# A decoder block on one core: token squares and decay columns later, the branch's split five gate tiles later, embedding norms from copies, the last two norms in two parts

## The chip, the cores and the metric

The kernel runs on one core of a Trainium2 chip. The time is the device time of one execution in microseconds (us), lower is better. TensorE multiplies matrices (its weight loads have their own row in the profile, PEld), VectorE (DVE), ScalarE (ACT) and GpSimd (POOL) do elementwise work, SyncE (SP) and POOL issue the DMA transfers. Matmul results lie in PSUM, in eight banks of 512 float32 columns; everything else lies in SBUF.

## The reference: one decoder layer

For a residual stream x of 512 tokens by 1024 channels the reference computes, in float32:

```
h = rms_norm(x, g_mix_pre);  z = h @ w_in          # 1024 -> 512 + 1024 + 1024 + 2048
y_pool = pool_mixer(z_pool) @ w_pool_out           # trailing means over 2, 4, 8, 16 tokens minus the token,
                                                   # each group through its 128x128 pool_w
y_rnn  = rg_lru_branch(z_rx, z_rg) @ w_rg_out      # conv of 4 taps, gates r and i, decay a = exp(-8 r softplus(-lambda)),
                                                   # linear scan over the tokens, times gelu(z_rg)
x = x + rms_norm((sigmoid(z_g1)*y_pool + sigmoid(z_g2)*y_rnn) @ w_o, g_mix_post)
up = rms_norm(x, g_ffn_pre) @ w_up                 # 1024 -> 2 x 3072
hid = gelu(causal_dwconv(up[:3072])) * up[3072:]
x = x + rms_norm(hid @ w_down, g_ffn_post)
ple = rms_norm(p @ w_ple_proj, g_ple_post)         # p: 512 x 256, the embedding of this layer
x = x + sigmoid(rms_norm(x, g_ple_gate) @ w_ple_gate) * ple
```

rms_norm divides by the root of the mean square over the 1024 channels of a token and multiplies by a gain. The reciprocal roots are called rstd below.

## The kernel before, in words

**Three passes for each product.** Every operand is split into two float32r numbers: `hi`, which is ScalarE's cast of the value, and `lo`, which is VectorE's difference between the value and `hi` (the subtraction in `sub`, line 189, called from `split` and from `prep`). A product is then three matmuls, hi by hi, hi by lo and lo by hi (`mm3`, lines 219 to 221). So each weight tile costs a DMA load by SP, a cast on ACT (line 433) and a subtraction on DVE (line 189) before TensorE may use its `lo`. `weight(key, ahead)` calls `prep` for so many tiles ahead of the one asked for, in the order of one list. The w_o, up and down products run as seven products of half-size blocks in place of eight, with sums and differences of the blocks formed in DRAM, in SBUF or in PSUM.

**What sets the order.** The program is written in one stream and a scheduler sorts each engine's instructions by priority; `tc.high_priority` and `urgent` move a stretch ahead, and `behind(ins, name)` forbids an instruction to stand ahead of another one of the same engine. Each engine then runs its list strictly in that order, so an instruction that waits holds up all that stand behind it.

**Start (lines 479 to 525).** SP loads x transposed in eight tiles of 256 KB (`m`, "x0" to "x7" below) and the four weight tiles of the recurrent input (`rx`, 512 KB). ACT scales each x tile into `hi` (line 487), DVE makes its `lo` (line 488), and TensorE runs eight steps k of twelve matmuls into four banks (line 524). Between these, SP loads x by tokens as well, in two transfers of 1 MB (`C<-x`, line 493), and ACT squares and sums them (line 507, four instructions). From the sums come the rstd of the tokens (POOL, line 455), and four diagonal matrices of them on DVE (line 515), which TensorE spreads to all partitions (line 569) in the first tile of the next product. On the same lines of work stand the decay columns `sp` of the recurrence, some 24 operations on 128x8 numbers on DVE and two on ACT (lines 544 to 563).

**Input projections (lines 578 to 750).** Twelve tiles `in` give the recurrent branch, then a written order `IN_ORDER` runs gate tiles, pool tiles and pool maps in turn. A gate or pool tile is 24 matmuls of 512 columns. A pool map is three matmuls: it multiplies the 128x128 block of `pool_w` (`hi_1423`, `lo_1424`) with the split trailing mean of a group. When the scans are done, `rnn_split` splits the eight results of the branch into `hi` and `lo` (the `C` tiles, eight casts and eight DVE subtractions); it is called behind gate tile 0.

**Mixer output and embedding (lines 765 to 1075).** Behind the w_o products come four tiles of the embedding (`ple_tile`, line 757): two products of 12 matmuls into two banks, a copy of one bank by DVE (line 769) and of the other by ACT (line 770), squares of both banks by ACT (line 462, in `rstd_of`), rstd on POOL, and the stores of the copies to DRAM. All squares but those of the start are kept in program order by `last_square`. Around these lie the norm of x after the mixer (`x2_sum`, `x2_out`: DVE lines 871, 874, 947) and the transposes of h2 on TensorE (line 879).

**End (lines 1188 to 1277).** `x3_norm(t, pair)` ends the down product for each tile of 128 tokens: `add_norm` multiplies both halves by the gain (line 871, two banks or a bank and an SBUF sum), squares both, takes the rstd and adds to the residual (line 874); then x3 times the next gain goes to `h` (line 1185), its squares give `r3`, and `x3_tile` transposes it on TensorE (line 879) and splits it. The last products run for h=0 and h=1, over t = 0 to 3, with the weights `wpg`, whose `lo` for h=1 is four DVE subtractions of 128x1024. `ple` tiles are multiplied by `rp` and the gain on DVE (line 1258), the sigmoid of the product is multiplied with them (1270), added to x3 (1271) and stored.

## Time and profile before

| what | before |
|---|---|
| three runs | 710.96, 711.29, 712.65 us; median 711.29 us |
| profiled execution | 712.31 us, of it span 710.3 us from the first to the last instruction |
| TensorE matmul | 699.5 us busy (98%), 4281 instructions |
| TensorE weight load | 637.0 us (90%) |
| VectorE | 576.6 us (81%) |
| ScalarE | 441.0 us (62%) |
| GpSimd | 82.3 us (12%) |
| DMA | 172.53 MB, mean 243 GB/s |

A busy time is the sum of an engine's instructions and does not say whether something waited for it. In a row of the timeline the first two numbers are start and duration in us; "xN" joins N neighbours of one kind; the bracket gives idle time before the row and what released it. In the list of waits the three numbers are total us, times, longest us. A matmul of 512 columns starts 0.216 us behind the one before it where nothing holds it, one of 256 columns 0.111 us; durations of matmuls overlap, so gaps are read from starts.

### The profile page before, as it was taken

The page shows a single profiled execution, that of the slowest core. Times are in us where ns is not written, and L with a number is a line of the kernel's source. Part 1 is how long each engine was busy: PE and PEld are TensorE (multiplying, and loading weights), DVE is VectorE, ACT ScalarE, POOL GpSimd, SP SyncE. Part 2 cuts the span into 40 slices and gives each one's busy share as a digit, 9 for nine tenths or more (in the row PEclk, how much of TensorE's full clock was granted, in tenths as well). Part 3 has the DMA queues.
Part 4 walks back from the last instruction along what each step waited for, and adds up shares of the span by engine and source line. Part 5 has one row for each costly group of instructions (what it writes and reads, how often), then busy time and mean ns, then how long its engine had stood idle before and what let it go on. Part 6 is the DMA issues. An engine that isn't in the chain of part 4 may idle for free.

```text
span 710.3 us, 11245 instructions
## 1 busy us (share of the span) xinstructions
PE 699.5 (98%) x4281; PEld 637.0 (90%) x4281; DVE 576.6 (81%) x749; ACT 441.0 (62%) x670; POOL 82.3 (12%) x107
## 2 busy tenths in 40 slices
PE   9999999999999999999999999999999999999897
PEld 7888888888888888889999999999999888888786
DVE  3897745999756578776989899899999999789852
ACT  6756789854643245487866677666667766574721
POOL 0311111110000000120013222222200000010100
PEclk9999999999999999999999999999999999999999
DMA  8999787765698999995379999999967677868011
GB/s 318 386 314 279 189 237 162 179 150 189 235 345 271 318 339 357 334 327 187 124 261 267 263 310 251 317 241 337 230 196 232 202 248 229 282 194 290 7 60 59
DMA packets 64933, 172.53 MB, mean 243 GB/s; under 512 B 5808, under 2 KB 6448, under 8 KB 64560
## 3 DMA queue, kind: packets, MB, share of 16 engines
q1 hardware_dynamic: 50336, 129.78, 52.7%
q0 software_dynamic: 14400, 41.95, 25.1%
q8 instruction: 33, 0.54, 0.3%
q14 instruction: 20, 0.16, 0.1%
q10 hardware_dynamic: 144, 0.10, 0.1%
HBM read 155.03 MB, written 58.72 MB: 301 GB/s over the span
## 4 chain that ended last, share of the span: by engine, by line
PE 75%; DVE 12%; ACT 5%; DMA 3%; issue 2%; POOL 1%; SPq 0%; DVEq 0%; POOLq 0%; ACTq 0%
PE ps L219 25%; PE ps L220 25%; PE ps L221 24%; DVE lo L189 3%; ACT m L164 1%; DMA C<-in_x_dram 1%; POOL s L455 1%; DVE m L656 1%; ACT t L164 1%; ACT rb L462 1%; DVE C L189 1%; DMA m<-in_x_t_dram 1%; DVE m L947 1%; PE ps L627 1%; DVE A L1258 1%
## 5 line engine op out<-in xcount | busy, mean ns | idle before, releaser
L189 DVE TENSOR_TENSOR lo<-raw,hi 128x1024 fp32r<-128x1024 f32 (+2 forms) x193 | 224.3, 1184 | 54.3 <-ACT hi L433 40.1
L219 PE MATMUL ps<-A,hi 128*128 128x256 f32 (+1 forms) x608 | 194.5, 320 | 0.0
L220 PE MATMUL ps<-A,hi 128*128 128x256 f32 (+1 forms) x608 | 193.8, 319 | 0.0
L221 PE MATMUL ps<-A,lo 128*128 128x256 f32 (+1 forms) x608 | 193.8, 319 | 0.0
L433 ACT CAST hi<-raw 128x1024 fp32r<-128x1024 f32 (+1 forms) x112 | 112.3, 1010 | 94.4 <-PE ps L220 28.3
L219 PEld LDWEIGHTS ps<-A,hi 128*128 128x128 f32 x608 | 115.9, 191 | 8.4 <-issue 1.3
L221 PEld LDWEIGHTS ps<-A,lo 128*128 128x128 f32 x608 | 116.0, 191 | 6.9
L220 PEld LDWEIGHTS ps<-A,hi 128*128 128x128 f32 x608 | 116.0, 191 | 6.7
L219 PE MATMUL ps<-C,hi 128*128 128x256 f32 (+1 forms) x392 | 114.7, 293 | 1.5 <-ACT rb L462 1.2
L220 PE MATMUL ps<-C,hi 128*128 128x256 f32 (+1 forms) x392 | 114.3, 291 | 0.0
L221 PE MATMUL ps<-C,lo 128*128 128x256 f32 (+1 forms) x392 | 114.3, 291 | 0.0
L193 ACT CAST hi<-raw 128x1024 fp32r<-128x1024 f32 x78 | 80.5, 1050 | 20.5 <-PE ps L220 12.2
L219 PE MATMUL ps<-hi,A 128*128 128x512 f32 x224 | 85.3, 381 | 0.0
L220 PE MATMUL ps<-lo,A 128*128 128x512 f32 x224 | 84.9, 379 | 0.0
L221 PE MATMUL ps<-hi,A 128*128 128x512 f32 x224 | 84.9, 379 | 0.0
L219 PEld LDWEIGHTS ps<-C,hi 128*128 128x128 f32 x392 | 74.7, 190 | 3.9 <-ACT rb L462 1.5
L220 PEld LDWEIGHTS ps<-C,hi 128*128 128x128 f32 x392 | 74.7, 191 | 1.8
L221 PEld LDWEIGHTS ps<-C,lo 128*128 128x128 f32 x392 | 74.7, 191 | 1.7
L455 POOL TENSOR_TENSOR s<-s,mhalf 128x1 f32<-128x1 f32 (+1 forms) x21 | 15.7, 749 | 343.0 <-DVE s L468 323.1
L219 PEld LDWEIGHTS ps<-hi,A 128*128 128x128 f32 x224 | 42.3, 189 | 6.3 <-ACT hi L433 0.3
L221 PEld LDWEIGHTS ps<-hi,A 128*128 128x128 f32 x224 | 42.3, 189 | 6.0
L220 PEld LDWEIGHTS ps<-lo,A 128*128 128x128 f32 x224 | 42.3, 189 | 5.9
(191 smaller groups left out, 1024.7 us busy)
## 6 DMA issues: line engine op xcount, KB each, us to landing
raw<-in_w_up_dram SPq DMA_DIRECT2D x46, 512.0 KB, 8.1
wdsum<-in_w_down_dram POOLq DMA_DIRECT2D x36, 512.0 KB, 9.1
raw<-in_w_in_dram SPq DMA_DIRECT2D x32, 512.0 KB, 7.1
raw<-wdsum SPq DMA_DIRECT2D x24, 512.0 KB, 4.2
raw<-in_w_down_dram SPq DMA_DIRECT2D x18, 512.0 KB, 4.4
wosum<-in_w_o_dram POOLq DMA_DIRECT2D x12, 512.0 KB, 9.7
wdsum<-wdsum POOLq DMA_DIRECT2D x12, 512.0 KB, 8.0
parts<-hi SPq DMA_DIRECT2D x10, 512.0 KB, 5.0
```

Of the source, the lines that this page charges most:

```text
L164: ins = ACT.activation(o, i, func, **kw)
L189: V.tensor_tensor(o, a, b, ALU.subtract)
L193: last_copy[0] = ACT.copy(hi, src)
L219: PE.matmul(o, ah, bh, start=start, stop=False, **kw)
L220: PE.matmul(o, ah, bl, start=False, stop=False, **kw)
L221: PE.matmul(o, al, bh, start=False, stop=stop, **kw)
L433: ACT.copy(hi, raw)
L455: last_pow[0] = nc.gpsimd.tensor_tensor(y, v, mhalf[:, :n], ALU.pow).ins.name
L462: ins = ACT.activation(rb, hsrc, AF.Square, scale=1.0 / 32.0, accum_out=s)
L627: PE.matmul(ps, bd[pr, a, o], turns(b[pr]), start=i == 0, stop=i == 2)
L656: V.tensor_tensor_scan(r, a_t[c], r, 0.0, ALU.mult, ALU.add)
L947: V.scalar_tensor_tensor(h2n[t, h], res[h], r, g_pre[h], ALU.mult, ALU.mult)
```

## The change

Five edits, which leave the sums and products as they are:

1. The two loads of x by tokens move behind the loads of the last weight tile and of x7; their squares may not stand ahead of the scaling of x5 (the first) and x7 (the other three). The four diagonals move behind `lo` of the weight tile `in` 0. The decay columns become a function that is called behind the third `in` tile.
2. `rnn_split` is called behind gate tile 5 in place of gate tile 0.
3. In the embedding the squares read the copies in SBUF in place of the banks, in a function `ple_norm` that is called behind the x2 work of the same tile; they leave the common order of squares.
4. `x3_norm` is split: `norm_of` squares one half while DVE multiplies the other half by the gain, and takes the rstd; `x3_add` does the rest. For t=2 and t=3 both adds come behind both `norm_of`, and the adds of t=2 not ahead of the last gain multiply of t=3.
5. The `ple` multiplies of t=2 and 3 may not stand ahead of the last multiply of x3; casts and subtractions of `wpg` for h=1 may not stand ahead of the last cast and the last subtraction of a `split`; the lookahead of `wpg` is cut to 3 - k//2 tiles for h=0, t=0 and 1.

```diff
-        V.tensor_tensor(o, a, b, ALU.subtract)
+        return V.tensor_tensor(o, a, b, ALU.subtract)
...
+        last_low[0] = sub(lo, src, hi.bitcast(F32)).ins.name
...
-            ACT.copy(hi, raw)
+            ins = ACT.copy(hi, raw)
+            if key[0] == "wpg" and key[2] == 1:
+                behind(ins, last_copy[0].ins.name)
...
-                sub(lo, raw, hi.bitcast(F32))
+                ins = sub(lo, raw, hi.bitcast(F32))
+                low_of[key] = ins.ins.name
+            if key[0] == "wpg" and key[2] == 1:
+                behind(ins, last_low[0])
...
+    def square(v, in_order=True):
+        s = tiny()
+        ins = ACT.activation(rb, v, AF.Square, scale=1.0 / 32.0, accum_out=s)
+        if in_order:
             if last_square[0] is not None:
                 behind(ins, last_square[0])
             last_square[0] = ins.ins.name
+        return s
...
+    def rstd_from(sums):
         v = tiny()
         V.scalar_tensor_tensor(v, sums[0], EPS, sums[1], ALU.add, ALU.add)
         return rsqrt(v)
...
         if k % 2 == 1 and k < 7:
-            if k > 1:
-                xt = quad("C", F32)
-                a = k // 2 - 1
-                nc.sync.dma_start(
...
             weight(("rx", k // 2 + 1), ahead=0)
+        if k in (5, 7):
+            load_tokens(k // 2 - 2)
...
+    last_func[0] = ht_done[-1]
...
-            ACT.activation(v, v, AF.Square, scale=1.0 / 32.0, accum_out=ssq[:, t : t + 1])
+            behind(ACT.activation(v, v, AF.Square, scale=1.0 / 32.0, accum_out=ssq[:, t : t + 1]), ht_done[7 if t else 5])
...
+        behind(V.tensor_scalar(diag[:, t * P : (t + 1) * P], ident, rstd1[:, t : t + 1], None, ALU.mult), low_of["in", 0])
...
+        if n == 2:
+            decay_columns()
...
-        if m == 0:
+        if m == 5:
             rnn_split()
...
-        s = rstd_of(pair)
...
+    def ple_norm(t, outs):
+        s = rstd_of(outs, in_order=False)
...
-            ple_tile(t)
+            outs = ple_tile(t)
...
+        ple_norm(t, outs)
...
+    def norm_of(pair, g):
+        og, sums = [temp(), temp()], []
+        for h in range(2):
+            sums.append(square(pair[h]))
+            ins = V.tensor_tensor(row(og[1 - h]), back(pair[1 - h]), row(g[1 - h]), ALU.mult)
+        return og, rstd_from(sums), ins.ins.name
...
+    def x3_add(t):
+        og, r, done = x3_first[t]
         res = [x3[t // 2][:, 2 * (t % 2) + h, :] for h in range(2)]
         with tc.high_priority(offset=URGENT if t > 1 else 0):
-            add_norm(pair, (gq[:, 0, :], gq[:, 1, :]), res)
+            norm_add(og, r, res, x3_first[3][2] if t == 2 else None)
...
+        if q == NQ + 1:
+            x3_add(2)
+            x3_add(3)
...
-            V.scalar_tensor_tensor(v, v, rp[t], gp[:, h, :], ALU.mult, ALU.mult)
+            ins = V.scalar_tensor_tensor(v, v, rp[t], gp[:, h, :], ALU.mult, ALU.mult)
+            if t > 1:
+                behind(ins, x3_last[0])
...
-                    w = weight(("wpg", k // 2, h))
+                    w = weight(("wpg", k // 2, h), ahead=AHEAD if h or t > 1 else 3 - k // 2)
```

TensorE's and POOL's instructions keep their order. On SP the two token loads and a few stores and loads behind the mixer change places. What moves on ACT and DVE is shown at three places. In a row stand line, operation, the output and the inputs; the numbers of buffers and lines differ between the two programs.

At the start, on ACT before (`A` is the scaling of an x tile, `C,s` a token square, the casts are those of rx tiles):

```order
L487 ACTIVATE A_131<-m_137,col 128x512
L487 ACTIVATE A_131<-m_138,col 128x512
L507 ACTIVATE C_173,s_201<-C_173 128x1024 x2
L433 CAST hi_177<-raw_175 128x1024
L487 ACTIVATE A_132<-m_139,col 128x512
L487 ACTIVATE A_132<-m_140,col 128x512
L507 ACTIVATE C_187,s_201<-C_187 128x1024 x2
L433 CAST hi_191<-raw_189 128x1024
L487 ACTIVATE A_132<-m_141,col 128x512
L487 ACTIVATE A_132<-m_142,col 128x512
```

and in the changed program:

```order
L506 ACTIVATE A_131<-m_137,col 128x512
L506 ACTIVATE A_131<-m_138,col 128x512
L433 CAST hi_175<-raw_173 128x1024
L506 ACTIVATE A_132<-m_139,col 128x512
L506 ACTIVATE A_132<-m_140,col 128x512
L433 CAST hi_187<-raw_185 128x1024
L521 ACTIVATE C_191,s_201<-C_191 128x1024
L506 ACTIVATE A_132<-m_141,col 128x512
L506 ACTIVATE A_132<-m_142,col 128x512
L521 ACTIVATE C_191,s_201<-C_191 128x1024
L521 ACTIVATE C_199,s_201<-C_199 128x1024 x2
L433 CAST hi_272<-raw_270 128x1024
```

The squares of the first two token tiles stood ahead of the rx cast and of x4 and x5, the other two ahead of the next rx cast and of x6 and x7. Now one square stands behind x5 and three behind x7.

On DVE around the first pool map, before (`C_1142` and `C_1152` are the low parts of the branch, `lo_1424` that of `pool_w`, `m_1304` that of the first pool group, `t` its running sums):

```order
L189 TENSOR_TENSOR C_1152<-m_996,C_1151 128x512
L189 TENSOR_TENSOR C_1152<-m_1002,C_1151 128x512
L712 TENSOR_TENSOR t_1297<-t_1294 128x512
L189 TENSOR_TENSOR lo_1424<-raw_1421,hi_1423 128x512
L189 TENSOR_TENSOR lo_1472<-raw_1469,hi_1471 128x1024
L189 TENSOR_TENSOR lo_1506<-raw_1503,hi_1505 128x1024
L717 SCALAR_TENSOR_TENSOR t_1299<-t_1297,t_1294 128x511
...
L189 TENSOR_TENSOR lo_1556<-raw_1553,hi_1555 128x1024
L189 TENSOR_TENSOR m_1304<-t_1299,m_1303 128x512
```

and in the changed program, where the low part of the first pool group is called `m_1284`:

```order
L189 TENSOR_TENSOR C_1402<-m_807,C_1401 128x512
L730 TENSOR_TENSOR t_1357<-t_1355 128x512
L189 TENSOR_TENSOR m_1284<-t_1279,m_1283 128x512
L599 TENSOR_TENSOR m_1318<-ps_1293,rb 128x512
...
L189 TENSOR_TENSOR m_1364<-t_1359,m_1363 128x512
L599 TENSOR_TENSOR m_1398<-ps_1373,rb 128x512
L189 TENSOR_TENSOR C_1412<-m_996,C_1411 128x512
L189 TENSOR_TENSOR C_1412<-m_1002,C_1411 128x512
L189 TENSOR_TENSOR lo_1424<-raw_1421,hi_1423 128x512
L189 TENSOR_TENSOR lo_1472<-raw_1469,hi_1471 128x1024
L189 TENSOR_TENSOR lo_1506<-raw_1503,hi_1505 128x1024
```

Before, all eight low parts of the branch stood ahead of the first pool group's chain, and `lo_1424` with two weights inside that chain. Now the chain of group 0 and most of that of group 1 (`t_1359`, `m_1364`) is interleaved with the low parts of the branch, `m_1284` stands ahead of the last five of these, and `lo_1424` and the four weights behind them all.

On DVE at the end, before, from the gain multiplies of t=3 on (`t<-ps` and `t<-sum`) to its `h` and the split of its transposes:

```order
L871 TENSOR_TENSOR t_6926<-ps_2822,C_5963 128x512
L871 TENSOR_TENSOR t_6928<-sum_6326,C_5963 128x512
L468 SCALAR_TENSOR_TENSOR s_6875<-s_6871,s_6873 128x1
L189 TENSOR_TENSOR lo_6958<-raw_6955,hi_6957 128x1024
L1188 COPY r_6879<-s_6877 128x1
L189 TENSOR_TENSOR lo_6970<-raw_6967,hi_6969 128x1024
L468 SCALAR_TENSOR_TENSOR s_6934<-s_6930,s_6932 128x1
L874 SCALAR_TENSOR_TENSOR C_6695<-t_6926,s_6936,C_6695 128x512
L874 SCALAR_TENSOR_TENSOR C_6695<-t_6928,s_6936,C_6695 128x512
L1185 TENSOR_TENSOR h_6809<-C_6695,C_5963 128x512 x2
L189 TENSOR_TENSOR h_7019<-ps_7020,h_7019 128x512
L189 TENSOR_TENSOR h_7019<-ps_7027,h_7019 128x512
```

and in the changed program, from the sum of squares of t=2 to the `h` of t=3 (`t_6912` and `t_6913` are the gain multiplies of t=3):

```order
L474 SCALAR_TENSOR_TENSOR s_6863<-s_6857,s_6860 128x1
L891 TENSOR_TENSOR t_6913<-sum_6326,C_5963 128x512
L189 TENSOR_TENSOR h_6867<-ps_6875,h_6867 128x512
L189 TENSOR_TENSOR lo_6903<-raw_6900,hi_6902 128x1024
L891 TENSOR_TENSOR t_6912<-ps_2822,C_5963 128x512
L896 SCALAR_TENSOR_TENSOR C_6695<-t_6855,s_6865,C_6695 128x512
L896 SCALAR_TENSOR_TENSOR C_6695<-t_6856,s_6865,C_6695 128x512
L1221 TENSOR_TENSOR h_6809<-C_6695,C_5963 128x512 x2
L474 SCALAR_TENSOR_TENSOR s_6920<-s_6914,s_6917 128x1
L896 SCALAR_TENSOR_TENSOR C_6695<-t_6912,s_6922,C_6695 128x512
L896 SCALAR_TENSOR_TENSOR C_6695<-t_6913,s_6922,C_6695 128x512
L1221 TENSOR_TENSOR h_6809<-C_6695,C_5963 128x512 x2
```

The weight subtractions `lo_6958` and `lo_6970`, which are the first for h=1, no longer stand between the gain multiplies of t=3 and its add, the gain multiplies of both tiles stand ahead of the adds of t=2, and the adds of both tiles follow one another.

More of the change, by code (lines that the diff above doesn't have):

```diff
@@ L456, in rsqrt @@
         return y
-    def rstd_of(halves):
-        sums = []
-        for hsrc in halves:
-            s = tiny()
-            ins = ACT.activation(rb, hsrc, AF.Square, scale=1.0 / 32.0, accum_out=s)
+    def square(v, in_order=True):
+        s = tiny()
+        ins = ACT.activation(rb, v, AF.Square, scale=1.0 / 32.0, accum_out=s)
+        if in_order:
             if last_square[0] is not None:
@@ L469, in rstd_of @@
         return rsqrt(v)
+    def rstd_of(halves, in_order=True):
+        return rstd_from([square(v, in_order) for v in halves])
     hth = [quad("A"), quad("A")]
@@ L479, in block_kernel, with load_tokens @@
     xtok = []
+    ht_done = []
+    def load_tokens(a):
+        xt = quad("C", F32)
+        nc.sync.dma_start(
+            xt.rearrange("p (a h) c -> p a (h c)", a=2),
+            x[2 * a * P : 2 * (a + 1) * P, :].rearrange("(a p) c -> p a c", p=P),
+        )
+        xtok.append(xt)
     for k in range(KD):
@@ L486, in block_kernel @@
         hi, lo = ht(k)
-        ht_done = ACT.activation(hi, raw, AF.Identity, scale=c1(C_GMIX + k)).ins.name
+        ht_done.append(ACT.activation(hi, raw, AF.Identity, scale=c1(C_GMIX + k)).ins.name)
         V.scalar_tensor_tensor(lo, raw, c1(C_GMIX + k), hi.bitcast(F32), ALU.mult, ALU.subtract)
         if k % 2 == 1 and k < 7:
-            if k > 1:
-                xt = quad("C", F32)
-                a = k // 2 - 1
-                nc.sync.dma_start(
-                    xt.rearrange("p (a h) c -> p a (h c)", a=2),
-                    x[2 * a * P : 2 * (a + 1) * P, :].rearrange("(a p) c -> p a c", p=P),
-                )
-                xtok.append(xt)
             weight(("rx", k // 2 + 1), ahead=0)
+        if k in (5, 7):
+            load_tokens(k // 2 - 2)
+    last_func[0] = ht_done[-1]
     ssq = tiny(NT)
@@ L512, in block_kernel @@
     sum_in_dram(chain_of(sums_of("wo"), sums_of("up")), None)
-    diag = temp()
-    for t in range(NT):
-        V.tensor_scalar(diag[:, t * P : (t + 1) * P], ident, rstd1[:, t : t + 1], None, ALU.mult)
     rx = [bank() for _ in range(4)]
@@ L524, in block_kernel @@
                 PE.matmul(rx[m], a[:, o : o + P], turns(b), start=k == 0 and i == 0, stop=k == KD - 1 and i == 2)
+    diag = temp()
+    for t in range(NT):
+        behind(V.tensor_scalar(diag[:, t * P : (t + 1) * P], ident, rstd1[:, t : t + 1], None, ALU.mult), low_of["in", 0])
     bd = quad("C").rearrange("p (s a) c -> p s (a c)", s=2)
@@ L770, in ple_tile @@
         ACT.copy(row(outs[1]), back(pair[1]))
-        s = rstd_of(pair)
+        for h, o in enumerate(outs):
+            nc.sync.dma_start(pled[t * P : (t + 1) * P, h * S : (h + 1) * S], o)
+        return outs
+    def ple_norm(t, outs):
+        s = rstd_of(outs, in_order=False)
         rp[t] = const.tile([P, 1], F32, tag=f"rp{t}", name=f"rp{t}")
         V.tensor_copy(rp[t], s)
-        for h, o in enumerate(outs):
-            nc.sync.dma_start(pled[t * P : (t + 1) * P, h * S : (h + 1) * S], o)
     def product(name, lhs, f, banks, start, head=0, tail=0):
@@ L864, in block_kernel, with norm_add @@
                 split(*pq[k], raw)
-    def add_norm(pair, g, res):
-        og = []
-        for h in range(2):
-            og.append(temp())
-            V.tensor_tensor(row(og[h]), back(pair[h]), row(g[h]), ALU.mult)
-        r = rstd_of(pair)
-        for h in range(2):
-            V.scalar_tensor_tensor(res[h], og[h], r, res[h], ALU.mult, ALU.add)
+    def norm_of(pair, g):
[4 more added lines that the diff above has]
+        return og, rstd_from(sums), ins.ins.name
+    def norm_add(og, r, res, after=None):
+        for h in range(2):
+            ins = V.scalar_tensor_tensor(res[h], og[h], r, res[h], ALU.mult, ALU.add)
+            if after is not None:
+                behind(ins, after)
+    def add_norm(pair, g, res):
+        og, r, _ = norm_of(pair, g)
+        norm_add(og, r, res)
     def transposed(a):
@@ L1177, in block_kernel @@
     x3n = {}
+    x3_first, x3_last = {}, [None]
     def x3_norm(t, pair):
+        with tc.high_priority(offset=URGENT if t > 1 else 0):
+            x3_first[t] = norm_of(pair, (gq[:, 0, :], gq[:, 1, :]))
+    def x3_add(t):
+        og, r, done = x3_first[t]
         res = [x3[t // 2][:, 2 * (t % 2) + h, :] for h in range(2)]
         with tc.high_priority(offset=URGENT if t > 1 else 0):
-            add_norm(pair, (gq[:, 0, :], gq[:, 1, :]), res)
+            norm_add(og, r, res, x3_first[3][2] if t == 2 else None)
             for h in range(2):
                 x3n[t, h] = nq[t // 2][:, 2 * (t % 2) + h, :]
-                V.tensor_tensor(x3n[t, h], res[h], gq[:, 2 + h, :], ALU.mult)
+                x3_last[0] = V.tensor_tensor(x3n[t, h], res[h], gq[:, 2 + h, :], ALU.mult).ins.name
         s3 = rstd_of(res)
@@ L1236, in block_kernel @@
             x3_norm(1, (c11[1], c12[1]))
+            x3_add(1)
             nq[1], gp = hquad(), hquad()
```

48 lines of the change are left out of this document (24 added, 24 removed).

## The prediction

> **What bounds the kernel now.** I read the page first, then TensorE's waits, then the timeline around each of them.
>
> ```profile
> PE 699.5 (98%) x4281; PEld 637.0 (90%) x4281; DVE 576.6 (81%) x749; ACT 441.0 (62%) x670; POOL 82.3 (12%) x107
> ```
> ```profile
> PE ps L879 <- DVE h L1185: 1.7, 1, 1.7
> PE ps L219 <- ACT rb L462: 1.2, 1, 1.2
> PE ps L237 <- DVE mhalf L231: 1.1, 1, 1.1
> PE ps L220 <- DVE m L189: 0.9, 1, 0.9
> PE ps L524 <- DVE lo L189: 0.7, 1, 0.7
> ```
>
> TensorE is the bound, and its list of matmuls does not change. All the change can win is stalls. There are few: the four rows beside the first wait of the program (L237) are one stall each, in four stages: the end, the embedding, the first pool map, the start. A stall costs its gap and then about 0.10 us, since the first matmul behind it starts its successor 0.32 us later in place of 0.216 (162.03 to 162.35 below). So each part is priced at its own stall, from starts of matmuls. I give all times on the clock of the profile before.
>
> **Part 1, the start.**
>
> ```profile
> 16.13 1.03 PE L524 MATMUL ps<-A,hi 128*128 128x512 f32 x4
> 17.35 1.13 PE L524 MATMUL ps<-A,hi 128*128 128x512 f32 x4 [0.20 <-ACT A L487]
> ...
> 21.77 1.90 PE L524 MATMUL ps<-A,hi 128*128 128x512 f32 x8
> 24.35 1.13 PE L524 MATMUL ps<-A,lo 128*128 128x512 f32 x4 [0.68 <-DVE lo L189]
> ```
> ```profile
> 13.55 1.06 ACT L507 ACTIVATE C<-C 128x1024 f32<-128x1024 f32 x1 [1.62 <-DMA C<-in_x_dram]
> ...
> 18.74 1.06 ACT L507 ACTIVATE C<-C 128x1024 f32<-128x1024 f32 x1 [0.83 <-DMA C<-in_x_dram]
> ```
> ```profile
> 22.28 0.88 DVE L515 TENSOR_SCALAR t<-ident,s 128x128 f32<-128x128 f32 x4 [1.15 <-POOL s L455]
> 23.08 1.21 DVE L189 TENSOR_TENSOR lo<-raw,hi 128x1024 fp32r<-128x1024 f32 x1
> ```
>
> Four matmuls from 16.13 make the next due at 16.99; it starts at 17.35, because x4's scaling stands behind two squares that waited for the token load (13.55). Eight from 21.77 make the next due at 23.50; it starts at 24.35, because the low part of the last rx tile (23.08) stands behind the diagonals, which waited for the second token load (18.74), two squares and POOL. Loss 0.36 + 0.85 + twice 0.10 = 1.4 us.
> Afterwards: between the rows 13.55 and 18.74 landed one rx tile, x4, x5 and the second token tile, 2 MB in 5.2 us, so 0.65 us per 256 KB. Without the first token load ahead of them (2.6 us), in the new order rx2 lands at 12.25, x4 12.9, x5 13.55, rx3 14.85, tokens 17.45, x6 18.1, x7 18.75, tokens 21.35. x4, x5 and rx3 are then scaled, cast and subtracted by 17.2, long before 22.2; both stalls go. What is late next: the diagonals. Two squares end at 23.45, DVE's sum and POOL take 1.4 (POOL's idle of DVE above is 1.15), so rstd is there at 24.8; two weight subtractions of 1.1 each stand ahead, three diagonals are done at 27.8, the fourth behind one more at 29.1. TensorE spreads them behind the twenty matmuls from 24.35 on and nine of the next product: 24.35 - 1.3 + 29 x 0.216 = 29.3. Margin 0.2, so the gain is 1.4, at worst 1.0. The 24 operations of the decay columns go to a stage in which DVE has idle time and gates start some 20 us later: nothing.
> The rows above agree with transfers that land in the order of issue. The Trainium skill, "DMA: Bandwidth & Descriptors", section "Queues, rings and completion order", says that completion is not first in, first out per issuing engine, and its section "Issuing engines are not separate DMA queues" that transfers interleave; by that the order of the loads alone would guarantee none of these landings. No row of this profile shows a load that overtakes another; the case in which one does is the third rival below.
>
> **Part 2, the branch's split.**
>
> ```profile
> 149.79 4.90 DVE L189 TENSOR_TENSOR C<-m,C 128x512 fp32r<-128x512 f32 x8
> ...
> 155.21 2.96 DVE L189 TENSOR_TENSOR lo<-raw,hi 128x512 fp32r<-128x512 f32 x3
> ```
> ```profile
> 160.74 0.38 PE L219 MATMUL ps<-m,hi 128*128 128x512 f32 x1
> 162.03 0.48 PE L220 MATMUL ps<-m,hi 128*128 128x512 f32 x1 [0.92 <-DVE m L189]
> 162.35 0.38 PE L221 MATMUL ps<-m,lo 128*128 128x512 f32 x1
> ```
> ```profile
> 130.00:165.00 35.00, 34.08 (x159) 29.52 (x158) 34.89 (x59) 20.86 (x32) 4.12 (x5) 1.00 0.70 186
> ```
>
> DVE is busy 34.89 of these 35 us: it is a queue that only order can shorten. The map's second matmul waits for `m_1304`, the last of its chain; due at 160.96, it starts at 162.03. With the new order `m_1284` comes early. Counting from 149.79, where the same work has been done in both, nine 512-wide rows at 0.61 (4.90/8) and two or three short ones stand up to and with `m_1284`: done by 155.7, five us before it is wanted. But the map's third matmul needs `lo_1424`, and this now stands behind all eight low parts and both chains: twenty 512-wide rows and some ten short ones, 20 x 0.61 + 0.4 = 12.6, so 162.4 where it was done by 155.9 (155.21, the first of the three). The third matmul, due at 161.17, runs at 162.35 as before. The wait changes its name and keeps its length. Then the next gate tile needs its own `lo_1472`, 1.13 later, at 163.5, where its third matmul was due at 163.0. So this part is no gain: -0.1 to -0.5, I take -0.4. Bounds: -0.6 with the restart, and +1.2 if the low parts are done early enough after all.
>
> **Part 3, the embedding norms.**
>
> ```profile
> 316.31 0.38 PE L221 MATMUL ps<-hi,m 128*128 128x512 f32 x1
> 316.89 0.38 PE L219 MATMUL ps<-C,hi 128*128 128x256 f32 x1 [0.21 <-ACT m L905]
> ```
> ```profile
> 322.68 0.71 PE L879 MATMUL ps<-ident,m 128*128 128x128 f32 x5
> 324.64 0.38 PE L219 MATMUL ps<-C,hi 128*128 128x256 f32 x1 [1.25 <-ACT rb L462]
> ```
> ```profile
> 323.09 1.28 DVE L769 COPY m<-ps 128x512 f32<-128x512 f32 x2
> ```
> ```profile
> 323.89 0.60 ACT L462 ACTIVATE rb<-ps 128x512 f32<-128x512 f32 x1 [2.02 <-DVE m L769]
> ```
>
> The 324.64 matmul writes a bank that is free only behind a copy on DVE (323.09) and then a square on ACT (323.89). The transposes' last start is near 323.12, so some 1.4 us go, 0.37 more at 316.89, and 0.1 for each restart: 2.0. With squares from the copies a bank is free once it is copied. What is late next are the copies themselves. ACT's copy of the last pair but one now stands behind two squares of the tile before, and I count it done at 322.3; DVE's keeps its place behind the norm's multiplies, so the first of the two at 323.09 ends at 323.7. TensorE, without its stalls, takes these two banks at 322.8 and 324.1. Margins of 0.5 and 0.4, and by the same count 0.3 at 316.9. I take 1.8 of the 2.0, and 1.0 if both slip. A square of a copy in SBUF is priced by the token squares of the start, 1.06 for 1024 columns, so 0.53 for 512, against 0.60 from a bank (323.89): no more than now, and ACT waits there anyway (2.02).
>
> **Part 4, the end.**
>
> ```profile
> 657.58 0.69 DVE L871 TENSOR_TENSOR t<-ps,C 128x512 f32<-128x512 f32 x1
> ...
> 671.08 1.41 DVE L874 SCALAR_TENSOR_TENSOR C<-t,s,C 128x512 f32<-128x512 f32 x2 [0.72 <-POOL s L455]
> 672.41 1.29 DVE L1185 TENSOR_TENSOR h<-C,C 128x512 f32<-128x512 f32 x2
> ```
> ```profile
> 665.06 0.38 PE L220 MATMUL ps<-lo,h 128*128 128x512 f32 x1
> 665.52 0.48 PE L221 MATMUL ps<-hi,h 128*128 128x512 f32 x1
> ```
> ```profile
> 671.03 0.38 PE L221 MATMUL ps<-hi,h 128*128 128x512 f32 x1
> 673.15 1.10 PE L879 MATMUL ps<-ident,h 128*128 128x128 f32 x6 [1.74 <-DVE h L1185]
> ```
>
> Stalls of 2.12 - 0.22 and 0.46 - 0.22, each with a restart: 2.3 us. In the new order the run on DVE from 657.58 to the `h` of t=3 is five gain multiplies or splits of 512 (0.6 to 0.7), one 1024-wide subtraction (1.13), four adds (1.33 per pair) and four `h` (1.2 per pair): 3.1 + 1.1 + 2.7 + 2.4 = 9.3, about 667 with POOL's rstd (0.72 idle above) hidden behind the adds of t=2. TensorE wants it at 671.2. A margin of 4 us holds for any slip here. The four weights for h=1 go behind this. I count them done from 677 to 681.6, 1.13 each between the last multiplies. TensorE wants the first behind the transposes at 673.15 (1.1 long, and 2.3 earlier without the stalls) and 48 matmuls: 673.15 + 1.1 - 2.3 + 10.4 = 682.3. Late, they would cost some 0.3. I take 2.3, bounds 1.8 and 2.4. The tail behind the last matmul keeps its work.
>
> **The sum.** 1.4 - 0.4 + 1.8 + 2.3 = 5.1. The profiled execution of 712.31 us (span 710.3 and 2.0 around it) becomes 707.2; it lies 1.0 above the median of 711.29, so against the median 5.1 less is 706.2.
>
> **The rivals.**
> 1. *The pool map's stall goes as well.* For it: `m_1284` is early. Against: the count for `lo_1424`. It adds 0.4 + 1.2: 704.6.
> 2. *A stage bound by DVE gives the early gains back.*
>
> ```profile
> 540.00:580.00 40.00, 40.00 (x226) 36.16 (x225) 39.86 (x40) 28.15 (x34) 0.00 (x0) 1.00 0.70 233
> ```
> ```profile
> 556.74 1.22 DVE L189 TENSOR_TENSOR A<-h,A 128x1024 fp32r<-128x1024 f32 x1
> ```
> ```profile
> 559.31 0.38 PE L219 MATMUL ps<-hi,A 128*128 128x512 f32 x1
> ```
> The operand of the down product that ends at 557.96 is used at 559.31, 1.35 later, and DVE has no idle there. If TensorE comes 2.8 earlier (1.4 - 0.4 + 1.8) and DVE does not, 1.45 come back: 707.7. If all before is lost, only part 4 stays: 709.0. Against: DVE's list is fed by TensorE's results before, and moves with it.
> 3. *Slower: the token tile lands with everything issued behind it.* Then ACT stops at the first token square, and the scaling of x6 and x7 stands behind it. Square and scaling take 1.06 and 0.67 us; TensorE wants x6 at 22.17 (x4 at 16.99, then two steps of twelve matmuls, 2.59 each). So from a landing at 20.4 on, each us later is a us lost. If that tile shares the bandwidth with all that is in flight behind it, some 4.5 MB at 2.6 us per MB from 14.85 on, it lands at 26.6: a loss of 6.2, part 1 becomes 1.4 - 6.2 = -4.8, and the sum -4.8 - 0.4 + 1.8 + 2.3 = -1.1: 712.4. The whole change turns into a loss from a landing at 25.5 on, and into one over 2.1 us at 27.6. Against: the rows 13.55 and 18.74 fit landing in order. The Trainium skill's page "DMA: Bandwidth & Descriptors" (section "Queues, rings and completion order") would allow this case; no row here shows it.
> 4. *The change does not do what it says in part 3.* Its margins are 0.3 to 0.5. If the norm's rstd is late, DVE's copies are. Part 3 falls to 0: 708.0; with half of part 1 and 0.3 of part 4 lost too, 709.
>
> **How the numbers follow.** My forecast has 0.55, the rivals 0.12, 0.15, 0.05 and 0.13. A measurement tells 0.3% from nothing, 2.1 us, so faster is below 709.2. The forecast, rival 1, four fifths of rival 2 and two thirds of rival 4 are: 0.55 + 0.12 + 0.12 + 0.09 = 0.88; I take 0.84, with 0.12 for within 0.3% (most of rival 3, the rest of rivals 2 and 4) and 0.04 for slower. The range holds the forecast's bounds and rivals 1, 2 and most of 4: 704.4 to 709.4.
>
> **What would show it.** Right: no gap of TensorE in its first 30 us beside the first weights; at the first pool map a wait of the third matmul for DVE's `lo`, not of the second for `m`; no wait for `rb` at the embedding; none for `h` at the end. Wrong: a wait of TensorE for the spread of the rstd (part 1), a wait for ACT's copies near 322 (part 3), a new wait between 340 and 640 (rival 2), or x6's scaling behind a token load (rival 3).

## The result and the profile after

The changed kernel takes 706.98 us (median of 4 runs, 706.74 to 707.59); on the same chip the kernel before takes 711.97 us (median of 4, 710.96 to 712.71). The ratio is 0.9932, with a 95% interval of 0.9915 to 0.9949: faster by 5.0 us, where 5.1 was forecast, at 706.98 against a forecast of 706.2. The profiled execution of the changed kernel took 707.59 us with a span of 705.8; before it was 712.31 and 710.3.

The page's busy times of the changed kernel:

```profile
PE 697.7 (99%) x4281; PEld 636.1 (90%) x4281; DVE 574.5 (81%) x749; ACT 440.9 (62%) x670; POOL 82.4 (12%) x107
```

TensorE's matmuls and their number are the same; its share of the span rose to 99%. Its waits in the changed kernel (what waits, for what, us in total, how often, the longest):

```profile
PE ps L221 <- DVE lo L189: 1.1, 2, 0.9
PE ps L237 <- DVE mhalf L231: 1.1, 1, 1.1
PE ps L534 <- ACT A L506: 0.6, 1, 0.6
PE ps L220 <- DVE C L189: 0.3, 1, 0.3
PE ps L534 <- ACT hi L430: 0.2, 1, 0.2
```

The waits for `h` (1.7), for `rb` (1.2) and for the `lo` of the start (0.7) are gone. The wait of the map's second matmul for `m` (0.9) has become one of a third matmul, L221, for `lo`, of the same length. New is 0.3 for `C`, at the embedding. The waits for `A` (0.6) and for the first `hi` (0.2) lie before 9.2 us: the first 10 us move with the landing of the first loads, by up to 1.0 us between the executions profiled here, and the two profiled executions are level again soon after (the matmuls that started at 16.13 before start at 16.20).

Both programs issue the same 4281 matmuls in the same order, so their starts can be subtracted one by one. What each stage won or lost in the two profiled executions ("won" is what a stage adds to the difference of the starts, the stages before it taken off):

| stage | before | after | won (+) | forecast |
|---|---|---|---|---|
| start: first matmul behind the twelve-matmul steps | 28.77 | 27.42 | +1.35 | +1.4 |
| pool map and next gate tile | 163.22 | 162.36 | -0.49 | -0.4 |
| a stall at 273 | | | -0.40 | 0 |
| embedding: first matmul behind the last transposes | 324.64 | 323.03 | +1.15 | +1.8 |
| 330 to 650, in small pieces | | | +0.31 | 0 |
| end: second half of the last transposes | 673.85 | 669.42 | +2.51 | +2.3 |
| sum | | | +4.43 | +5.1 |

The start, on ACT (start, us, then the operation; what the idle time before it waited for is in brackets):

```profile
17.57 1.06 ACT L521 ACTIVATE C<-C 128x1024 f32<-128x1024 f32 x1 [1.54 <-DMA C<-in_x_dram]
...
21.45 1.06 ACT L521 ACTIVATE C<-C 128x1024 f32<-128x1024 f32 x1 [0.47 <-DMA C<-in_x_dram]
```

The token loads landed at 17.57 and 21.45; counted were 17.45 and 21.35. The next thing to be late, the diagonals, on DVE and then their use on TensorE:

```profile
28.61 0.28 DVE L539 TENSOR_SCALAR t<-ident,s 128x128 f32<-128x128 f32 x1
```
```profile
29.36 0.83 PE L585 MATMUL ps<-t,m 128*128 128x128 f32 x6
```

The fourth diagonal is done at 28.89, 0.47 before the first spread. The margin was put at 0.2.

The first pool map and the gate tile behind it, on TensorE and on DVE:

```profile
159.61 0.38 PE L220 MATMUL ps<-m,hi 128*128 128x512 f32 x1
160.90 0.48 PE L221 MATMUL ps<-m,lo 128*128 128x512 f32 x1 [0.91 <-DVE lo L189]
...
162.04 0.48 PE L221 MATMUL ps<-A,lo 128*128 128x512 f32 x1 [0.22 <-DVE lo L189]
```
```profile
153.42 0.68 DVE L189 TENSOR_TENSOR m<-t,m 128x512 fp32r<-128x512 f32 x1
...
160.17 4.09 DVE L189 TENSOR_TENSOR lo<-raw,hi 128x512 fp32r<-128x512 f32 x4
```

`m` is ready at 154.1, over five us before it is wanted. But `lo_1424`, the first of the four rows from 160.17, is done at 160.86 and the map's third matmul starts then; on the clock of before that is 162.2, where 162.4 was counted. The gate tile's third matmul waits for its own `lo` for another 0.22.

The embedding, on TensorE:

```profile
314.52 0.38 PE L221 MATMUL ps<-hi,m 128*128 128x512 f32 x1
314.96 0.48 PE L219 MATMUL ps<-hi,m 128*128 128x512 f32 x1
...
316.89 0.38 PE L220 MATMUL ps<-C,hi 128*128 128x256 f32 x1 [0.26 <-DVE C L189]
...
322.24 1.04 PE L907 MATMUL ps<-ident,m 128*128 128x128 f32 x8
323.03 0.36 PE L219 MATMUL ps<-C,hi 128*128 128x256 f32 x1
```

The matmul that stood at 324.64 behind `rb` runs at 323.03 with no wait. Two small stalls appeared in front of it: the matmul at 314.96 was due at 314.73 (0.22 behind the one before), and the one at 316.89 waits 0.26 for a low part. With their restarts they cost 0.34 and 0.40. What feeds them on DVE:

```profile
313.55 0.75 DVE L975 SCALAR_TENSOR_TENSOR m<-m,s,m 128x512 f32<-128x512 f32 x1 [0.66 <-POOL s L460]
314.22 0.68 DVE L891 TENSOR_TENSOR t<-ps,m 128x512 f32<-128x512 f32 x1
...
316.15 1.28 DVE L189 TENSOR_TENSOR C<-ps,C 128x512 fp32r<-128x512 f32 x2
```

L891 is the gain multiply of `norm_of`, which reads a bank; it ends at 314.90, and the matmul of 314.96 takes a bank behind it. The low parts at 316.15 end at 316.8 and 317.4.

The end, on DVE and on TensorE:

```profile
664.31 1.29 DVE L1221 TENSOR_TENSOR h<-C,C 128x512 f32<-128x512 f32 x2
```
```profile
668.76 0.38 PE L221 MATMUL ps<-hi,h 128*128 128x512 f32 x1
668.98 1.04 PE L907 MATMUL ps<-ident,h 128*128 128x128 f32 x8
```

`h` of t=3 is done at 665.60, and TensorE goes from its last matmul into the transposes without a gap, 3.4 us later (4 was counted).

### The profile page after: what moved, and what is told of

It reads as the page before. It is cut to its first block, busy times and chain, and to the rows that moved or that the text cites. A ratio compares the mean times of both kernels' runs of the same rounds, so it can differ in the third digit from the quotient of the medians.

```text
span 705.8 us, 11240 instructions
## 1 busy us (share of the span) xinstructions
PE 697.7 (99%) x4281; PEld 636.1 (90%) x4281; DVE 574.5 (81%) x749; ACT 440.9 (62%) x670; POOL 82.4 (12%) x107
## 4 chain that ended last, share of the span: by engine, by line
PE 85%; DVE 7%; ACT 4%; DMA 2%; issue 1%; SPq 0%; POOL 0%; DVEq 0%; ACTq 0%
PE ps L219 27%; PE ps L221 27%; PE ps L220 27%; PE ps L534 3%; ACT m L164 2%; DVE m L672 1%; ACT t L164 1%; DMA raw<-wosum 1%; PE ps L907 1%; DMA m<-in_x_t_dram 1%; DVE C L189 1%; PE ps L643 1%; DVE lo L189 1%; DVE m L671 1%; ACT hi L433 1%
## 5 line engine op out<-in xcount | busy, mean ns | idle before, releaser
L221 PE MATMUL ps<-A,lo 128*128 128x256 f32 (+1 forms) x608 | 193.9, 319 | 0.2 <-DVE lo L189 0.2
L221 PEld LDWEIGHTS ps<-A,lo 128*128 128x128 f32 x608 | 116.0, 191 | 7.5 <-DVE lo L189 0.6
L221 PE MATMUL ps<-C,lo 128*128 128x256 f32 (+1 forms) x392 | 114.2, 291 | 0.0
L221 PE MATMUL ps<-hi,A 128*128 128x512 f32 x224 | 85.0, 379 | 0.1
L221 PEld LDWEIGHTS ps<-C,lo 128*128 128x128 f32 x392 | 74.7, 190 | 1.7
L221 PEld LDWEIGHTS ps<-hi,A 128*128 128x128 f32 x224 | 42.3, 189 | 6.5 <-DVE A L189 0.5
```

The source lines that it names most:

```text
L221: PE.matmul(o, al, bh, start=False, stop=stop, **kw)
```

## The experiments

Each kernel is the changed kernel with one thing, or one group of things, undone or altered; none leaves out a part of the computation. Times are medians. Each ratio is against runs of the kernel before on the same chip (712.1 to 712.4 us); the changed kernel's own ratio is 0.9932, and 0.001 is 0.7 us. Waits and shifts come from one profiled execution each, with matmuls compared one by one as above.

**The branch split as early as before, all else as changed.**

```diff
-        if m == 5:
+        if m == 0:
             rnn_split()
```

> The changed kernel with the branch's split behind gate tile 0 again (part 2 undone, all else kept). Theory A (the later split costs: the pool map keeps its 1.1 us wait under another name, gate tile 8 gains a wait of 0.4, and the low parts, the early weight splits and their stores behind them come later, which is what TensorE meets as 0.4 us at 273): the second matmul of the first pool map waits again for DVE's m, 1.1 us; no wait at gate tile 8 (-0.5 us); no wait at 273 (-0.4 us); time about 706.1, 0.9 below the changed kernel. Theory B (the 0.4 us at 273 come from TensorE being earlier against a chain fed by DMA, wherever the split is): the wait at 273 stays, or grows to 0.9 since TensorE gets there 0.5 earlier; time 706.5 to 707.0.

Measured: 706.5 us (4 runs, 705.94 to 706.72), ratio 0.9925 (0.9908 to 0.9941). Its wait:

```profile
PE ps L220 <- DVE m L189: 0.9, 1, 0.9
```

The map's second matmul waits for `m` again, the gate tile's wait is gone, and TensorE is 0.47 earlier by 162. By the trace part 2 of the change costs some 0.5 us and wins nothing; the times alone can't tell it, since the two ratios' intervals overlap. The stall at 273 is gone too; the kernels below show that the split does not decide this.

**The branch split two tiles later still.**

```diff
-        if m == 5:
+        if m == 7:
             rnn_split()
```

> The changed kernel with the split called behind gate tile 7 (two gate tiles later still). On DVE the low part of pool_w then stands directly behind the first pool sum, and the low parts of the branch are spread between the pool chains. Theory A (the pool map waits for whatever low part comes last in this queue): no wait at the first pool map or gate tile 8, 1.6 us less there; a wait of 0 to 0.3 at the third pool map, whose chain I count done at 171.4 against 171.2 wanted. If nothing behind gives it back: about 705.4. Theory B (the stretch 200 to 275 is set by DMA and by stores that free buffers, not by TensorE): most of the 1.6 is lost again at 273, where a wait of 1.5 to 2.0 us appears; time 706.7 to 707.0.

Measured: 705.11 us (4 runs, 704.69 to 705.37), ratio 0.9903 (0.9889 to 0.9918). The same place, on DVE and on TensorE:

```profile
148.90 1.83 DVE L189 TENSOR_TENSOR lo<-raw,hi 128x512 fp32r<-128x512 f32 x2
...
154.34 0.69 DVE L189 TENSOR_TENSOR m<-t,m 128x512 fp32r<-128x512 f32 x1
```
```profile
159.44 0.38 PE L220 MATMUL ps<-m,hi 128*128 128x512 f32 x1
159.66 0.38 PE L221 MATMUL ps<-m,lo 128*128 128x512 f32 x1
```

`lo_1424`, the first of the two from 148.90, is done at 149.6, ahead of all low parts of the branch, and `m` at 155.0, with one of them ahead of it. The map runs through: 1.67 us are won by 163, where rival 1 was priced at 1.6, and they are kept to the end. The small wait that was expected at the third pool map did not come. The stall was one of order alone: DVE has the time, and the split stood two tiles too early for it.

**The embedding's squares from the banks again, in order, inside the tile.**

```diff
-        for h, o in enumerate(outs):
-            nc.sync.dma_start(pled[t * P : (t + 1) * P, h * S : (h + 1) * S], o)
-        return outs
-
-    def ple_norm(t, outs):
-        s = rstd_of(outs, in_order=False)
+        s = rstd_of(pair)
```

> The changed kernel with the embedding's squares as before: from the banks, in the common order of squares, inside the embedding tile (part 3 undone). Theory A (a bank is held by copy and square, and that was the stall): the wait of TensorE for ACT's rb at 323 is back with 1.0 to 1.5 us, the two smaller waits at 314 and 316 (0.33 and 0.4) go or change; time about 708.1, 1.1 above the changed kernel. Theory B (the gain at 324 came from the new form of the norm of x, squares first, which is kept here): no wait for rb over 0.3; time within 0.4 of 707.0.

Measured: 709.88 us (6 runs, 708.61 to 711.35), ratio 0.9968 (0.9953 to 0.9982).

```profile
PE ps L219 <- ACT rb L465: 2.2, 1, 2.2
```

The wait for `rb` is back, and with 2.2 us it is longer than before (1.2): TensorE reaches its transposes 1.62 us earlier than in the kernel before (320.73), while DVE's two copies, and the square behind them, come only 0.63 earlier (322.46 in place of 323.09). The stage loses 2.3 us by the trace. So the squares are what made the stall, and in the new program they would cost more than part 3 has won. The medians differ by 2.9 us; two of the six runs (710.4 and 711.35) had a mean granted clock of 0.996, and the undone end below shows what a pause of this length can do to the clock.

**The squares from the copies, but at the old place and in order.**

```diff
         ACT.copy(row(outs[1]), back(pair[1]))
+        ple_norm(t, outs)
...
-        s = rstd_of(outs, in_order=False)
+        s = rstd_of(outs)
...
-        ple_norm(t, outs)
```

> The changed kernel with the embedding's squares reading the copies in SBUF, but at their old place: inside the embedding tile and in the common order of squares. Theory A (what counts is that the square no longer holds the bank): no wait of TensorE for rb at 323; up to 0.5 us more at 314 to 317, since the gain multiply that frees a bank moves back on DVE; 706.8 to 707.6. Theory B (what counts is the place, squares behind the work on x): the wait near 323 is back with 1 us or more, 708 or over.

Measured: 707.58 us (4 runs, 707.14 to 708.03), ratio 0.9939 (0.9924 to 0.9954). No wait for `rb` at 323, so it is the source of the square that frees the bank, not its place. But the squares now stand ahead of an ACT copy that TensorE needs at 315:

```profile
PE ps L219 <- ACT m L934: 1.2, 1, 1.2
```

The stage loses 0.65 net. Both halves of the edit do work: the source takes away the first stall, the place keeps a second one off.

**The whole end undone: old norm form and order for x3, weights for h=1 early.**

```diff
-            if key[0] == "wpg" and key[2] == 1:
-                behind(ins, last_low[0])
...
-            norm_add(og, r, res, x3_first[3][2] if t == 2 else None)
+            plain_norm(pair, (gq[:, 0, :], gq[:, 1, :]), res)
...
-                    w = weight(("wpg", k // 2, h), ahead=AHEAD if h or t > 1 else 3 - k // 2)
+                    w = weight(("wpg", k // 2, h))
```

(`plain_norm` is the form of before: both gain multiplies, then both squares. The order of the embedding's multiplies is undone with it.)

> The changed kernel with the whole of its end undone: x3's norm in one piece and in its old form (gain multiplies first, then the squares), no order between the embedding multiplies, the weights of h=1 and the norm, the old lookahead. Theory A (part 4 is worth its two stalls): waits of TensorE for h at the last transposes, 1.7 to 1.9, and a small one near 663; time 709.3 to 709.6, 2.3 to 2.6 above the changed kernel, all of it behind 660. Theory B (half of it came from TensorE's earlier arrival or from elsewhere): under 1.5 above, below 708.5.

Measured: 710.37 us (10 runs, 709.15 to 712.28), ratio 0.9974 (0.9959 to 0.9989).

```profile
PE ps L913 <- DVE h L1220: 1.7, 1, 1.7
...
PE ps L221 <- DVE h L189: 0.7, 1, 0.7
```

The stall of 1.7 is back. By the trace the two stalls cost 1.20 and 2.16, 3.4 in all; 0.4 come back at 273, which has no stall here, and some tenths in the first 10 us. Five of the runs (709.15 to 709.85, mean granted clock 0.999 or 1.0) lie 2.2 to 2.9 us above the changed kernel, as that says. The other five (clock 0.997 or 0.998) took 710.9 to 712.28. In the profiled execution, one of these, more is lost behind the stall. Windows of that kernel (length, busy time of TensorE, weight loads, DVE, ACT, POOL; then granted clock, DMA share, GB/s), and TensorE's rows there:

```profile
671.00:674.00 3.00, 2.65 (x12) 2.15 (x13) 2.73 (x6) 2.93 (x7) 0.80 (x1) 0.77 0.00 0
674.00:676.00 2.00, 2.00 (x6) 1.58 (x5) 1.84 (x4) 0.00 (x0) 0.13 (x1) 0.50 0.08 29
```
```profile
671.31 1.32 PE L913 MATMUL ps<-ident,h 128*128 128x128 f32 x8 [1.74 <-DVE h L1220]
...
673.63 0.63 PE L219 MATMUL ps<-hi,h 128*128 128x512 f32 x1
674.05 0.63 PE L220 MATMUL ps<-lo,h 128*128 128x512 f32 x1
```

Behind the 1.74 us pause and the transposes the clock is granted at 0.50, and for about 3.4 us the matmuls start 0.43 apart (673.63, 674.05) in place of 0.216. That costs another 1.7 us, nearly as much as the stall itself.

**The pause filled.** As above, with seven 512-wide matmuls on tiles that are long ready, written into the bank that the transposes then overwrite.

```diff
-    def transposed(a):
+    def transposed(a, fill=0):
         ps = bank()
+        for _ in range(fill):
+            PE.matmul(ps, x3t[1, 0][0][:, :P], x3t[1, 1][0], start=True, stop=True)
...
-            ps = transposed(x3n[t, h])
+            ps = transposed(x3n[t, h], 7 if (t, h) == (3, 0) else 0)
```

> The kernel with the whole end undone (709.2 to 712.3 in ten runs) and seven matmuls of 512 columns more, on tiles that lie ready, into the bank of the last transposes ahead of them (they are overwritten): 7 x 0.216 = 1.5 us of work inside the wait of 1.7 us for h. The output is the same. Theory A (after a pause of this length TensorE is granted half its clock in some executions, which costs up to 2 us more, and this is why the runs lie from 709.2 to 712.3): with the pause filled the clock stays at 1.00 and all runs lie between 709.0 and 710.2. Theory B (the spread has another cause): runs up to 711 and more as before, or about 1.5 us added to all if the filling does not lie inside the wait.

Measured: 709.5 us (6 runs, 708.89 to 711.26), ratio 0.9957 (0.9931 to 0.9983). The mean granted clock of the six runs is 0.999 or 1.0, where five of the ten above had 0.997 or 0.998, and in the profiled one the clock behind the transposes is granted at 1.00. That supports the clock as the cause of the second loss. The profiled run, 710.29 us, has no second loss: its stalls at 663 and at the transposes cost 0.74 and 2.2 against the changed kernel's trace, and behind them it runs 1.6 us ahead of the undone end's. It does not prove it: one of the six runs took 711.26 us at a clock of 0.999, and where its time went stays open.

**The x3 norm in one piece, late weights and new form kept.**

```diff
-            norm_add(og, r, res, x3_first[3][2] if t == 2 else None)
+            add_norm(pair, (gq[:, 0, :], gq[:, 1, :]), res)
```

(`add_norm` is the new form for one tile, here with tile 2 finished ahead of tile 3. The order of the embedding's multiplies is undone with it.)

> The changed kernel with x3's norm in one piece again (tile 2 finished before tile 3) and without the order of the embedding multiplies; the new form (square and gain multiply of the two halves in exchange) and the later weights of h=1 stay. Theory A (either the later weights or the split is enough for TensorE's 3.4 us of margin at the last transposes): h of t=3 is done at about 667.5, wanted at 669.0, no wait over 0.3; time 707.0 within 0.4. Theory B (the split is what carries part 4): a wait for h of 1 us or more, time over 708.

Measured: 708.58 us (6 runs, 708.3 to 710.15), ratio 0.9952 (0.9937 to 0.9967).

```profile
671.37 0.48 PE L221 MATMUL ps<-hi,h 128*128 128x512 f32 x1 [0.78 <-DVE h L189]
```

No expectation had this quite right. The transposes of t=3 come only 0.25 and 0.20 late, for the two halves of `h`, but a matmul behind them waits longer, for the low part of `h`; the end loses 1.58 us. Of the 2.5 of part 4 the two parts of the norm carry the most.

**The weights for h=1 early, norm in two parts kept.**

```diff
-                    w = weight(("wpg", k // 2, h), ahead=AHEAD if h or t > 1 else 3 - k // 2)
+                    w = weight(("wpg", k // 2, h))
```

(The two `behind` for these weights and the one for the embedding's multiplies are taken out with it.)

> The changed kernel with the weights of h=1, the embedding multiplies and the lookahead at their old order; the split of x3's norm and the new form stay. Two weight subtractions (2.3 us) stand again inside the norms. Theory A (margin): h of t=3 ends at 665.6 + 2.3 = 667.9, wanted at 669.0: no wait; 707.0 within 0.4. Theory B (these weights were the cause of the long wait): a wait for h of 1 us or more, time over 708.

Measured: 707.44 us (4 runs, 706.7 to 708.0), ratio 0.9934 (0.9915 to 0.9953). By the trace the end loses 0.4 at 670.6, to a low part; `h` is still in time, but barely: its two halves are done at 668.66 and 669.26, some 0.3 and 0.2 us before their transposes, where the changed kernel has `h` whole 3.4 us before the first one (669.0 less 665.6). The order of the weights is worth 0.4 and a margin.

**The start undone: token loads, squares, diagonals and decay columns at their old places.**

```diff
+            if k > 1:
+                xt = quad("C", F32)
...
-        if k in (5, 7):
-            load_tokens(k // 2 - 2)
...
-    def decay_columns():
```

> The changed kernel with part 1 undone: token loads, squares, diagonals and decay columns at their places in the kernel before. Theory A (the two waits at 17 and 24 us are what part 1 removed): waits of TensorE for ACT's A near 17 and for DVE's lo near 24, 1.35 us together with their restarts; time about 708.3 (1.3 above the changed kernel). Theory B (TensorE's first 10 us vary between executions by 0.9 us with the first loads, and that is as much as part 1 gives): the waits are there, but the median differs by less than 0.7, under 707.7.

Measured: 708.57 us (5 runs, 708.01 to 708.59), ratio 0.9949 (0.9933 to 0.9965).

```profile
PE ps L533 <- DVE lo L189: 0.7, 1, 0.7
PE ps L533 <- ACT A L496: 0.5, 2, 0.3
```

Both old stalls return at their old places (of the two waits for `A` the one at 17.33 is 0.17, the other lies in the first 10 us), and 1.39 us are lost by 25: part 1 is worth what was counted. They are kept to the end, but for the 0.40 of the stall at 273, which this kernel does not have.

**Only the token loads at their old places; squares, diagonals and decay columns late.**

```diff
+        if k in (3, 5):
+            load_tokens(k // 2 - 1)
...
-        if k in (5, 7):
-            load_tokens(k // 2 - 2)
```

> The changed kernel with the two token loads issued at their old places, ahead of the last two rx tiles; squares, diagonals and decay columns stay late. Theory A (ACT's order was the wait, since squares stood ahead of x's scaling; the loads only move x4 to 15.5 and the last rx tile to 20.0, wanted at 17.0 and 23.0): a wait of 0 to 0.5 near 17, 707.0 to 707.5. Theory B (the transfers themselves held x back): 0.8 to 1.4 of the start's gain are lost, 707.8 to 708.4.

Measured: 707.99 us (4 runs, 707.49 to 708.18), ratio 0.9943 (0.9926 to 0.9959). No stall at 17 or 24, but this one at the spread, which is due at 29.4 and starts at 30.2:

```profile
PE ps L585 <- DVE t L539: 0.7, 1, 0.7
```

The loss is 0.94, by a mechanism that neither expectation named. With the tokens ahead of it the last rx tile is cast only at 20.1, x7 scaled by 22.4, and the three late squares end at 25.4. The cast of the next weight stands behind them on ACT, three subtractions on DVE wait for that cast, and the diagonals behind them start at 29.9 where the spread wants them at 29.4. It is the step "what is late next" of part 1, with its margin of 0.5 used up. The order of the loads is needed for that margin. The two stalls go without it, by the order of squares, diagonals and decay columns; which of these does it was not tried apart.

**Split at 7, and the x2 norms in the form of before.**

```diff
-        if m == 5:
+        if m == 7:
             rnn_split()
...
     def add_norm(pair, g, res):
-        og, r, _ = norm_of(pair, g)
-        norm_add(og, r, res)
+        og = []
+        for h in range(2):
+            og.append(temp())
+            V.tensor_tensor(row(og[h]), back(pair[h]), row(g[h]), ALU.mult)
+        r = rstd_of(pair)
+        for h in range(2):
+            V.scalar_tensor_tensor(res[h], og[h], r, res[h], ALU.mult, ALU.add)
```

> The changed kernel with the branch's split behind gate tile 7 (705.1 alone) and the norm of x after the mixer in its old form (gain multiplies of both halves first, then the squares); the last norms keep the new one. Theory A (the two small waits at 314 and 316, 0.33 and 0.40 us, come from the new form, which puts a gain multiply and half of the norm's output ahead of the multiply that frees a bank and ahead of h2's low part on DVE): both go, 704.4. Theory B (they are there in any order, since DVE is behind there): 705.1, or a wait of TensorE for rb near 323 in their place, over 706.

Measured: 704.81 us (4 runs, 704.33 to 706.41), ratio 0.9904 (0.9888 to 0.9921), span 702.4. Against the split at 7 alone TensorE wins 0.8 between 312 and 315, where both small stalls of the embedding go. The only row that its waits have left:

```profile
PE ps L237 <- DVE mhalf L231: 1.1, 1, 1.1
```

In time it can't be told from the split at 7 alone (705.11). The runs of both (704.33 to 706.41) lie below the fastest of the changed kernel (706.74).

## Why the prediction was right, step by step

**The sum.** 5.1 was forecast and 5.0 measured in the medians; the trace has 4.43. The nearness of 5.0 is partly chance, since three terms missed: part 3, the stall at 273 and the small gains behind 330. The 0.6 between 4.43 and 5.0 is no stage's: the two profiled executions differ by 4.72, of it 0.26 outside the spans, and the changed kernel's lies 0.61 above its median, that of before 0.34.

**Part 1** was right in size and in mechanism. The token loads landed within 0.12 us of the count, both stalls went (1.35 of 1.4), and the diagonals are what is late next; the margin was 0.47, not 0.2. Undoing it costs 1.39. Rival 3, the token tile that lands with everything behind it, is refuted here: the Trainium skill, "DMA: Bandwidth & Descriptors", section "Queues, rings and completion order", says that completion is not first in, first out, but these loads landed as the count in the order of issue has them. In the traces of before and after, every load that SP issues in the first 20 us lands in the order of issue (x6 at 18.21, behind the first token load at 17.54).

**Part 2** was right: a wait that changes its name and keeps its length, then a second one at the next gate tile, -0.49 against -0.4. Rival 1, that the stall goes as well, did not happen, but the split at 7 shows that its mechanism works from two tiles later on.

**Part 3** was right in mechanism and wrong in size. The step that failed is the one on the margins: "by the same count 0.3 at 316.9. I take 1.8 of the 2.0". That margin slipped, and a stall at 314.96 came that no step named: 0.34 and 0.40. The copies near 322 and 323.7 held. The square of a copy was priced too low, at 0.53; it takes 0.63 (the rows of ACT at 323.95 and 324.71), but TensorE waits for none of them. What was not priced is that `add_norm`, which the x2 tiles use in this stage, takes the new form too; with the old form for x2 both stalls are gone and 0.8 us are won. The term measured 1.15. Rival 4 named the direction, but priced it at all of the 1.8; 0.65 were lost.

**A stall at 273** was not foreseen, and its cause is not settled. There a matmul waits for a low part on DVE, 0.40 with its restart in the changed kernel. In the kernel with early weights two wait, one for ACT and one for that low part, 1.35 together. In the other kernels none does, and in five of them ACT, DVE, POOL and SP have the same order of instructions up to that point as in these two: squares from the banks, squares at the old place, end undone, pause filled, norm in one piece. ACT's waits for the stores of split weights, between 200 and 275, before and then after (us in total, how often, the longest):

```profile
ACT hi L433 <- DMA parts<-hi: 21.2, 5, 5.8
```
```profile
ACT hi L433 <- DMA parts<-hi: 27.1, 5, 7.0
```

They were 28.3 in the kernel with early weights (up to 276), and 18.5 to 22.3 in the five of the same order, which have no stall. So among kernels of one order it goes with how late these stores end. But it doesn't follow from that alone: with the branch split as early as before the waits are 27.0, with the start undone 27.4, and neither has a stall there. That the stores cause it is argued, and why they end later was not tried.

**Rival 2** (DVE gives early gains back) did not happen: between 330 and 650 TensorE won another 0.31, and the 1.7 of the split at 7 were kept to the end.

**Part 4** was right: 2.51 against 2.3. Undone alone, the two parts of the norm are worth 1.6 and the late weights 0.4; both keep the new form, in which one half is multiplied while the other is squared, and undoing all three costs 3.4.

**What the parts don't do** is add up when undone one by one: 1.4 + 2.3 + 3.4 - 0.5 = 6.6 is over the 4.43 of the whole. Stalls that were small before are longer when one part is put back into the new program: 2.2 for `rb` where it was 1.2, and 0.7 for the low part of `h` where the matmul lost 0.24. For `rb` the row of that experiment says why: TensorE comes 1.62 us earlier to a square that comes 0.63 earlier. For the rest it was not traced.

## What to carry to other kernels

When a stall waits for the last item of a busy in-order engine, list what stands ahead of each operand the next few matmuls need: moving one item up moves the wait to the next operand, unless the block goes behind all that would wait, as nearly all of it does with the split at 7. A helper whose form is changed for one place has to be priced at every place that calls it. Squares taken from a copy free a bank one operation earlier, but where they stand among the copies matters as much.

## What the runs showed of the hardware

A pause of TensorE can cost twice. The rows of the undone end show matmuls at half rate for about 3.4 us, with the granted clock at 0.50, behind a pause of 1.74 us (2.12 between the starts of two matmuls); the execution of before that was profiled had the same pause and kept its clock. The Trainium skill, "TensorE: Matmul & The Clock Gate", section "HAM oscillation — how this bites in real kernels", puts the limit at gaps of about 3.4 us; here, with the eight small transposes behind it, a shorter one was enough in the one execution that was traced with such a stretch. It would fit the spread of the kernel before as well: of 33 of its runs, 12 had a mean granted clock of 0.998 or less and a median of 713.2 us, and 21 had 0.999 or more and a median of 711.7. A mean of 0.998 alone is weak evidence: the profiled run of the kernel with squares at the old place has it too, and there the clock is at 0.50 only in the last 2.4 us, where no matmul is left. Seven of the 33 runs had 0.997, with a median of 713.7. How much of the 5.0 us between the medians comes from such stretches no run shows.
